# The low halves of the attention's weights, made on GpSimd in place of VectorE

## The chip, the core and the metric

The kernel runs on one core of a Trainium2 chip. The time is device time in microseconds (us), of whole executions. The engines are called by the profile's names: PE is TensorE's matmul (PEld its weight load), DVE is VectorE, ACT is ScalarE, POOL is GpSimd, SP is SyncE, which issues most loads. TensorE's granted clock stands as PEclk, 1.00 being 2.4 GHz.

## What is computed

Two transformer blocks, one behind the other, on 512 tokens of width 1024. The first has a convolution branch, a spatial gating branch and a mixture of 32 experts; the second has a feed-forward layer, a mixer of two attentions and a second feed-forward layer. The change touches the mixer of the second block alone:

```python
h = rmsnorm(x, g_mix[l])
p = h @ w_in[l]
qa, ka, va, qi, ki, wi, cq, ckv, kr = jnp.split(p, split_points, axis=-1)
...
out_a = dsa_sparse_attention(qa, ka, va, qi, ki, wi)
out_b = mla_attention(cq, ckv, kr, g_q_lat[l], g_kv_lat[l], w_uq[l], w_ukv[l], cos_b, sin_b)
x = x + jnp.concatenate([out_a, out_b], axis=-1) @ w_out[l]
```

The sparse attention (DSA) scores every earlier token with 16 small index heads, keeps the best 128 of them for each query, and attends to these alone. The latent attention (MLA) makes its queries, keys and values from two narrow projections (`cq`, `ckv`) and attends to all earlier tokens. Both outputs go through one projection.

## The kernel before

It is written in a tile framework: the program calls operations on named tiles, the framework finds the dependences, sets the waits and puts each engine's instructions into one order at build time, mostly that of the program, with later work moved ahead where a planner expects an engine to be free. On the chip each engine runs its queue strictly in that order.

**Split products.** A matmul in single pass rounds its operands. To keep accuracy, an operand is split into a high half (rounded) and a low half (the rest), and a product is three matmuls (`mm3`, lines 254 to 259): low by high, high by low, high by high, in this order. `hilo` (L201) makes the halves: ACT copies the source into the rounded type (L203, CAST in the profile), then DVE subtracts that from the source (L204). The same two lines serve weights and activations; in the profile the weights' halves are the tiles `wh` and `wl`, the activations' are called `t`.

**Weight stream.** `Stream` (L87) walks over a list of weight tiles: it lets SP load raw tiles four ahead of their use, and calls `wtile` (L219) two ahead, which takes a `wh` and a `wl` buffer (three of each, L128) and calls `hilo`. So the cast of a tile waits until PE is done with the tile three places before.

**The attention** (`attention`, L1209) runs these stages. The first stream (`st`, L1222) has 20 tiles: one of the key projection, eight for the index queries (1040 columns each, two to a group of heads), seven for keys and latents, four for the sparse attention's queries (1024 columns). The row scales come from `rms` (L326, with `rsqrt`, L261). For each group of index heads, `project`, `rotate` (rotary, L1274 to 1286) and `score_qi` (L1317) follow; `score_qi` adds the heads' scores up with one DVE instruction for each head and block (L1329). Then come the latent projections (L1353), the value projection with a tile of its own (L1398), and the stream `st2` (L1412) with 12 narrow tiles (four of 256, eight of 384 columns) for the MLA heads. `heads` (L1563) runs eight heads of one kind: scores with mask and maximum on DVE (L1520), exponentials on ACT (L1524), transposes and copies (L1537 to 1542), products with the values (L1550).

`choose` (L1453) finds the best 128 scores in 16 rounds of two DVE instructions (L1458, L1459). The order puts many of them early, as filling between other DVE work. `project_out` (L1477) takes the eight tiles of the output projection from the stream `st3` (L1475): four of them, for the MLA half, in between the last rounds, the others two by two at the end (L1498, L1499). The second feed-forward layer begins right behind, with a stream of its own.

Of the kernel before, what the change touches and what calls it, by code (L numbers as in the profile page):

```python
# [7 lines left out]
F32 = mybir.dt.float32  # L8
# [3 lines left out]
ALU = mybir.AluOpType  # L12
# [63 lines left out]
class Blocks:  # L76


    def __init__(self, tiles, n, w=512):
        self.tiles, self.n, self.w, self.per = tiles, n, w, 2048 // w  # L80
# [37 lines left out]
class Net:  # L118
    def __init__(self, tc, ctx, A, out):
        self.tc, self.nc, self.A, self.out, self.ctx = tc, tc.nc, A, out, ctx  # L120
        nc = self.nc
        ec = ctx.enter_context
        self.own = None
        self.const = ec(tc.tile_pool(name="const", bufs=1))
        self.p8 = ec(tc.tile_pool(name="p8", bufs=16))
        self.p4 = ec(tc.tile_pool(name="p4", bufs=4))
        self.p2 = ec(tc.tile_pool(name="p2", bufs=5))
        self.wp = ec(tc.tile_pool(name="wp", bufs=3))  # L128
        self.sm = ec(tc.tile_pool(name="sm", bufs=2))
        self.pp = ec(tc.tile_pool(name="pp", bufs=8, space=PSUM))  # L130
        self.dr = ec(tc.tile_pool(name="dr", bufs=1, space=DRAM))
        c = self.const
        self.x = c.tile([128, ND, T], F32, name="x")
        self.vec = c.tile([128, NV], F32, name="vec")
        nc.scalar.dma_start(self.vec, A["vec"])
        self.cc = c.tile([128, NC_], F32, name="cc")
        nc.scalar.dma_start(self.cc, A["cc"])
        self.ident = self.cc[:, C_ID:C_ID + 128]
        self.ones = c.tile([128, 128], F32, name="ones")
        nc.vector.memset(self.ones, 1.0)  # L140
        self.table = self.dr.tile([ROUNDS * 128 * NE, 4], I32, name="table")
        self.ordd = self.dr.tile([1, NE], I32, name="ordd")
        self.hrow = self.dr.tile([T, D], F32, name="hrow")
        self.pay = c.tile([128, NT, 2, 4], I32, name="pay")
        self.br = c.tile([128, NG + NE], F32, name="br")
        self.order = c.tile([128, NE], I32, name="order")
        self.payf = c.tile([128, NT, NFIXED, 4], F32, name="payf")
        self.payi = c.tile([128, NT, 2], F32R, name="payi")
        self.g12 = c.tile([128, ND], F32, name="g12")
        o1, o2 = VOFF["norm_final_g"], VOFF["g_ffn1_2"]  # L150
        nc.vector.tensor_tensor(self.g12, self.vec[:, o1:o1 + ND], self.vec[:, o2:o2 + ND], op=ALU.mult)
# [46 lines left out]
    def blocks(self, n, dt=F32, w=512):  # L198
        return Blocks([self.t8([128, 2048], dt) for _ in range(-(-n * w // 2048))], n, w)

    def hilo(self, hi, lo, src):  # L201
        nc = self.nc
        nc.scalar.copy(hi, src)  # L203
        nc.vector.tensor_tensor(lo, src, hi.bitcast(F32), op=ALU.subtract)  # L204

    def half(self, hi, lo, src, g):

# [11 lines left out]
    def wtile(self, view):  # L219

        shape = list(view.shape)
        if self.own is not None:
            wh, wl = (w.rearrange("p a b -> p (a b)").rearrange("p (a b) -> p a b", b=shape[2])
                      for w in self.own["w"].pop(0))
            self.hilo(wh, wl, view)
            return wh, wl
        wh = self.wp.tile(shape, F32R, name="wh", tag="wh")
        wl = self.wp.tile(shape, F32R, name="wl", tag="wl")
        self.hilo(wh, wl, view)
        return wh, wl  # L230

    def stream(self, items, loads=4, ahead=2):
# [976 lines left out]
    def attention(self):  # L1209
        nc, A = self.nc, self.A  # L1210
        mul, add, sub = ALU.mult, ALU.add, ALU.subtract
        def tok_items(nm, w, c):
            return [((nm, c), self.load8(w[c]), (lambda r, h=h: r[:, 4 * h:4 * h + 4, :])) for h in range(2)]
# [5 lines left out]
        items += self.stat_items("wf", wf, range(1, 8))  # L1219
        for c in range(2):  # L1220
            items += tok_items("qa", wqa, c)
        st = self.stream(items)  # L1222
        st.split(2)
        xh, xl = self.halves(lambda k: self.v("g_mix_2", k))
# [252 lines left out]
        def project_out(j, cs):  # L1477

            ws = [next(st3) for c in cs]
            accs = [self.ps() for m in range(2 * len(cs))]  # L1480
            for n, k in enumerate(ks[j]):
                for m, acc in enumerate(accs):
                    (wh, wl), o = ws[m // 2], slice(m % 2 * 128, m % 2 * 128 + 128)
                    self.mm3(acc, (wh[:, n, o], wl[:, n, o]), (mh[k], ml[k]), n == 0, n == 3)
            for m, acc in enumerate(accs):
                xm = self.x[:, 2 * cs[0] + m, :]
                nc.vector.tensor_tensor(xm, acc, xm, op=add)
# [9 lines left out]
        self.heads(dsa)  # L1497
        project_out(1, (0, 1))  # L1498
        project_out(1, (2, 3))  # L1499

    PO = [0, 128, 384, 768]
    SO = [0, 512, 896, 1152]
# [206 lines left out]
```

## Time and profile before

| | |
|---|---|
| median of three runs | 2027.65 us (2027.0 to 2028.92) |
| profiled execution, its own time | 2028.41 us |
| its span, first to last instruction | 2026.5 us |
| PE busy in the span | 1918.1 us, 95% |
| DVE busy | 1293.8 us, 64% |
| ACT busy | 715.6 us, 35% |
| POOL busy | 48.4 us, 2%, 69 instructions |
| mean granted clock | 0.978 |

The busy shares are means over stages that have little in common, so the attention has to be read by itself: how long each engine is busy in each of its stages, what PE waits for there, and where the subtractions stand in DVE's queue. A busy PE is one with at least one matmul under way; matmuls overlap, so that the step from one start to the next is shorter than one matmul's duration.

### The profile page before, as it was taken

The page shows a single profiled execution, that of the slowest core. Times are in us where ns is not written, and L with a number is a line of the kernel's source. Part 1 is how long each engine was busy: PE and PEld are TensorE (multiplying, and loading weights), DVE is VectorE, ACT ScalarE, POOL GpSimd, SP SyncE. Part 2 cuts the span into 40 slices and gives each one's busy share as a digit, 9 for nine tenths or more (in the row PEclk, how much of TensorE's full clock was granted, in tenths as well). Part 3 has the DMA queues.
Part 4 walks back from the last instruction along what each step waited for, and adds up shares of the span by engine and source line. Part 5 has one row for each costly group of instructions (what it writes and reads, how often), then busy time and mean ns, then how long its engine had stood idle before and what let it go on. Part 6 is the DMA issues. An engine that isn't in the chain of part 4 may idle for free.

```text
span 2026.5 us, 24440 instructions
## 1 busy us (share of the span) xinstructions
PE 1918.1 (95%) x9375; PEld 1428.8 (71%) x9375; DVE 1293.8 (64%) x2234; ACT 715.6 (35%) x1116; POOL 48.4 (2%) x69
## 2 busy tenths in 40 slices
PE   7999999979998899887999999999989999999997
PEld 5898888867554353332788888887867788888886
DVE  7999997457777575555754442459999755444323
ACT  5334325345343221111532322336366633223221
POOL 0000001003000000000000000000000000000000
PEclk9999999988999999999999999999999999999998
DMA  6121232527999999998232224130111122222311
GB/s 258 53 87 60 104 124 104 236 108 271 385 409 409 408 416 408 410 420 334 85 104 94 94 79 170 66 151 1 53 50 47 48 83 92 96 94 83 151 57 42
DMA packets 60087, 341.59 MB, mean 169 GB/s; under 512 B 8208, under 2 KB 9168, under 8 KB 27456
## 3 DMA queue, kind: packets, MB, share of 16 engines
q1 hardware_dynamic: 55152, 329.87, 42.2%
q0 software_dynamic: 3520, 6.35, 1.0%
q10 hardware_dynamic: 1296, 3.79, 0.5%
q8 instruction: 74, 1.21, 0.2%
q14 instruction: 45, 0.37, 0.1%
HBM read 339.37 MB, written 4.54 MB: 170 GB/s over the span
## 4 chain that ended last, share of the span: by engine, by line
PE 47%; DVE 3%; ACT 2%; issue 0%; DMA 0%; DVEq 0%; ACTq 0%; SPq 0%
PE ps L257 15%; PE ps L259 14%; PE ps L258 14%; PE ps L1550 1%; ACT t L1524 1%; PE ps L1537 1%; DVE wl L204 0%; DVE t L204 0%; PE ps L1292 0%; ACT wh L203 0%; PE ps L1555 0%; DVE t L1520 0%; ACT t L203 0%; PE ps L295 0%; PE ps L1293 0%
## 5 line engine op out<-in xcount | busy, mean ns | idle before, releaser
L257 PE MATMUL ps<-t,wl 128*128 128x512 f32 x1728 | 684.2, 397 | 18.7 <-ACT t L208 18.3
L258 PE MATMUL ps<-t,wh 128*128 128x512 f32 x1728 | 681.2, 394 | 0.9 <-DVE t L209 0.9
L259 PE MATMUL ps<-t,wh 128*128 128x512 f32 x1728 | 681.4, 394 | 0.0
L203 ACT CAST wh<-t 128x1024 fp32r<-128x1024 f32 (+3 forms) x321 | 324.9, 1017 | 716.9 <-PE ps L259 532.7
L204 DVE TENSOR_TENSOR wl<-t,wh 128x1024 fp32r<-128x1024 f32 (+3 forms) x321 | 378.3, 1183 | 212.0 <-ACT wh L203 208.8
L257 PEld LDWEIGHTS ps<-t,wl 128*128 128x128 f32 x1728 | 325.3, 188 | 96.9 <-ACT t L208 19.1
L258 PEld LDWEIGHTS ps<-t,wh 128*128 128x128 f32 x1728 | 326.0, 189 | 76.8 <-DVE t L209 2.3
L259 PEld LDWEIGHTS ps<-t,wh 128*128 128x128 f32 x1728 | 325.3, 188 | 75.4
L257 PE MATMUL ps<-wh,t 128*128 128x256 f32 (+2 forms) x440 | 147.4, 337 | 23.2 <-DVE t L204 23.2
L972 PE MATMUL ps<-t,t 128*32 128x512 f32 (+1 forms) x832 | 162.6, 606 | 5.5 <-DMA t<-in_w_up 3.6
L403 DVE SCALAR_TENSOR_TENSOR t<-t,vec,t 128x512 f32<-128x512 f32 x240 | 165.7, 745 | 0.4
L1025 DVE TENSOR_TENSOR x<-x,ps 128x512 f32<-128x512 f32 x200 | 126.4, 683 | 44.9 <-PE ps L1024 44.1
L258 PE MATMUL ps<-wl,t 128*128 128x256 f32 (+2 forms) x440 | 145.7, 331 | 0.0
L259 PE MATMUL ps<-wh,t 128*128 128x256 f32 (+2 forms) x440 | 144.4, 328 | 0.0
L257 PEld LDWEIGHTS ps<-wh,t 128*128 128x128 f32 x440 | 85.8, 195 | 33.0 <-DVE t L204 25.1
L972 PEld LDWEIGHTS ps<-t,t 128*32 128x32 f32 (+1 forms) x832 | 41.4, 123 | 91.7 <-issue 78.8
L1181 DVE TENSOR_TENSOR t<-ps,rbc 128x512 f32<-128x512 f32 x44 | 30.4, 690 | 115.6 <-PE ps L259 115.6
L259 PEld LDWEIGHTS ps<-wh,t 128*128 128x128 f32 x440 | 85.9, 195 | 7.4
L258 PEld LDWEIGHTS ps<-wl,t 128*128 128x128 f32 x440 | 86.0, 195 | 6.8
L1024 PEld LDWEIGHTS ps<-t,t 128*128 128x128 f32 x248 | 42.8, 190 | 67.1 <-issue 31.6
L1024 PE MATMUL ps<-t,t 128*128 128x512 f32 x248 | 78.7, 424 | 11.5 <-DVE t L1012 7.4
L203 ACT CAST t<-t 128x512 fp32r<-128x512 f32 (+2 forms) x102 | 62.7, 619 | 57.5 <-DVE t L1182 26.2
(317 smaller groups left out, 1597.1 us busy)
## 6 DMA issues: line engine op xcount, KB each, us to landing
t<-in_w_down SPq DMA_DIRECT2D x80, 1024.0 KB, 19.8
t<-in_w_gate SPq DMA_DIRECT2D x64, 1024.0 KB
t<-in_w_up SPq DMA_DIRECT2D x64, 1024.0 KB, 19.2
t<-in_w_in SPq DMA_DIRECT2D x24, 1024.0 KB, 4.7
t<-in_w_gate SPq DMA_DIRECT2D x44, 512.0 KB
t<-in_w_up SPq DMA_DIRECT2D x44, 512.0 KB, 3.4
t<-in_w_down SPq DMA_DIRECT2D x8, 768.0 KB, 11.4
t<-in_w_qi SPq DMA_DIRECT2D x4, 1040.0 KB, 4.7
```

The source lines that it names most:

```text
L203: nc.scalar.copy(hi, src)
L204: nc.vector.tensor_tensor(lo, src, hi.bitcast(F32), op=ALU.subtract)
L257: mm(acc, a[1], b[0], start=first, stop=False)
L258: mm(acc, a[0], b[1], start=False, stop=False)
L259: mm(acc, a[0], b[0], start=False, stop=last)
L403: nc.vector.scalar_tensor_tensor(y[c], src, w, y[c], op0=mul, op1=add)
L972: nc.tensor.matmul(p[o:o + c, :], xT[:, k * CAP + i:k * CAP + i + c], w[:, q, :], start=k == 0, stop=k == ND - 1)
L1024: self.nc.tensor.matmul(p, yT[:, k * 128:k * 128 + 128], sel, start=j == 0, stop=j == n - 1)
L1025: self.nc.vector.tensor_tensor(self.x[:, k, :], self.x[:, k, :], p, op=ALU.add)
L1181: nc.vector.tensor_tensor(a, accs[1], rbc, op=mul)
L1524: nc.scalar.activation(part(i), part(i), AF.Exp, bias=nm[:, i:i + 1], scale=scale, accum_out=su[:, i:i + 1])
L1537: nc.tensor.transpose(tb[b][:, o + (i - s) * 128:o + (i - s) * 128 + 128], P[:, self.PO[i] + s * 128:self.PO[i] + s * 128 + 128], self.ident)
```

## The change

`hilo` gets an argument for the engine that makes the low half; only `wtile` passes one, from a field of the net. `attention` sets the field to GpSimd ahead of its first stream and clears it at its end, so that the 41 weight tiles of the attention (20 of the first stream, the value projection's one, 12 narrow ones and eight of the output projection) have their low halves made there. The casts stay on ACT, and the activations' low halves on DVE. All other streams of the kernel are as before.

```diff
@@ -118,6 +118,7 @@
 class Net:
     def __init__(self, tc, ctx, A, out):
         self.tc, self.nc, self.A, self.out, self.ctx = tc, tc.nc, A, out, ctx
+        self.low = None
         nc = self.nc
@@ -198,10 +199,10 @@
-    def hilo(self, hi, lo, src):
+    def hilo(self, hi, lo, src, low=None):
         nc = self.nc
         nc.scalar.copy(hi, src)
-        nc.vector.tensor_tensor(lo, src, hi.bitcast(F32), op=ALU.subtract)
+        (low or nc.vector).tensor_tensor(lo, src, hi.bitcast(F32), op=ALU.subtract)
@@ -226,7 +227,7 @@
         wl = self.wp.tile(shape, F32R, name="wl", tag="wl")
-        self.hilo(wh, wl, view)
+        self.hilo(wh, wl, view, self.low)
         return wh, wl
@@ -1219,6 +1220,7 @@
         for c in range(2):
             items += tok_items("qa", wqa, c)
+        self.low = nc.gpsimd
         st = self.stream(items)
         st.split(2)
@@ -1497,6 +1499,7 @@
         project_out(1, (0, 1))
         project_out(1, (2, 3))
+        self.low = None
```

## Rows read from the trace of the kernel before

**Rows 1.** Busy time by stage (stretch, length, then each engine, clock, DMA).

```profile
core 0: us, PE busy (x) PEld busy (x) DVE busy (x) ACT busy (x) POOL busy (x), PEclk, DMA share, GB/s
1300.00:1350.00 50.00, 50.00 (x252) 42.23 (x252) 22.37 (x26) 18.64 (x24) 0.00 (x0) 1.00 0.33 126
1350.00:1430.00 80.00, 73.72 (x444) 63.31 (x443) 71.46 (x146) 43.87 (x95) 0.00 (x0) 0.98 0.13 51
1430.00:1480.00 50.00, 49.85 (x333) 44.91 (x333) 48.13 (x137) 15.81 (x25) 0.00 (x0) 1.00 0.04 12
1480.00:1550.00 70.00, 60.80 (x333) 47.38 (x333) 66.08 (x171) 55.77 (x133) 0.00 (x0) 0.95 0.15 49
1550.00:1585.00 35.00, 34.94 (x193) 27.13 (x191) 31.82 (x82) 13.22 (x30) 0.00 (x0) 1.00 0.19 69
```

**Rows 2.** Waits, 1350 to 1585 us: us in total, times, the longest.

```profile
PE ps L257 <- DVE t L204: 7.1, 3, 4.7
...
DVE wl L204 <- ACT wh L203: 4.6, 6, 1.6
```

**Rows 3.** Groups by line and shape, DVE, 1325 to 1645: busy, mean ns.

```profile
L204 DVE TENSOR_TENSOR wl<-t,wh 128x1024 fp32r<-128x1024 f32 x23 | 28.0, 1219 | 7.7 <-ACT wh L203 7.5
...
L204 DVE TENSOR_TENSOR wl<-t,wh 128x384 fp32r<-128x384 f32 x8 | 4.4, 552 | 0.6 <-ACT wh L203 0.6
```

**Rows 4.** DVE's busy time on the weights' low halves alone, by stage.

```profile
1350.00:1430.00 80.00, 11.08 (x9) 0.98 0.13 51
1430.00:1480.00 50.00, 9.46 (x9) 1.00 0.04 12
1480.00:1550.00 70.00, 7.80 (x13) 0.95 0.15 49
1550.00:1585.00 35.00, 4.66 (x4) 1.00 0.19 69
```

**Rows 5.** Groups by line and shape, POOL, whole span.

```profile
L565 POOL TENSOR_SCALAR t<-t,vec 128x36 f32<-128x36 f32 x8 | 2.8, 365 | 2.2 <-DMA t<-in_w_router 2.2
...
L559 POOL MEMSET t<- 128x2048 f32 x1 | 1.8, 1810 | 22.3 <-DVE wl L204 22.3
...
L391 POOL MEMSET t<- 128x96 f32 x3 | 0.6, 186 | 38.6 <-DVE t L376 28.3 <-DVE wl L204 10.3
...
L669 POOL CAST ur<-ones 128x128 fp32r<-128x128 f32 x1 | 0.3, 292 | 0.0
```

**Rows 6.** Timeline of ACT in the score stage: start, us.

```profile
1360.64 1.06 ACT L203 CAST wh<-t 128x1040 fp32r<-128x1040 f32 x1 [0.62 <-PE ps L259]
...
1364.97 1.07 ACT L203 CAST wh<-t 128x1040 fp32r<-128x1040 f32 x1 [1.21 <-PE ps L259]
```

**Rows 7.** Timelines of DVE and PE at the last weight tile.

```profile
1632.48 1.22 DVE L204 TENSOR_TENSOR wl<-t,wh 128x1024 fp32r<-128x1024 f32 x1
...
1633.84 0.47 PE L257 MATMUL ps<-t,wl 128*128 128x512 f32 x1
```

**Rows 8.** Timeline of DVE in the chain of the row scales.

```profile
1351.32 1.24 DVE L204 TENSOR_TENSOR wl<-t,wh 128x1040 fp32r<-128x1040 f32 x1
1352.48 0.17 DVE L269 RECIPROCAL r<-rs 128x4 f32<-128x4 f32 x1
1352.68 0.16 DVE L270 TENSOR_TENSOR rt<-r 128x4 f32<-128x4 f32 x1
```

**Rows 9.** Timeline of all engines, 339 us, in the first block.

```profile
339.05 0.75 DVE L482 SCALAR_TENSOR_TENSOR t<-ps,vec,t 128x512 f32<-128x512 f32 x1
339.27 0.29 POOL L668 CAST ur<-cc 128x128 fp32r<-128x128 f32 x1 [13.90 <-ACT t L203]
```

**Rows 10.** Groups by line, DVE, 1350 to 1585 us: those with two SBUF inputs.

```profile
L1329 DVE SCALAR_TENSOR_TENSOR t<-t,wb,t 128x256 f32<-128x256 f32 (+2 forms) x45 | 24.6, 614 | 0.3 <-ACT t L1326 0.2
...
L204 DVE TENSOR_TENSOR t<-t,t 64x512 fp32r<-64x512 f32 (+2 forms) x22 | 15.0, 681 | 0.2
L1280 DVE TENSOR_TENSOR t<-t 128x256 f32<-128x256 f32 x20 | 8.4, 418 | 0.1
```

## The prediction

> **What bounds the kernel now.** I read the views in this order: the busy time by stage, the waits of the attention, the weights' rows on VectorE (DVE), and then single stretches of the timeline. The attention runs from about 1350 to 1645 us, and its first two weight tiles are made a little earlier. Up to 1350 TensorE (PE) never stops: 50.00 busy of 50.00 us, with DVE at 22.37. Nothing that DVE gives up there can be worth anything. Behind that the picture changes [rows 1]. PE stands for 80 - 73.72 = 6.28 us in the score stage (1350 to 1430), for 0.15 us in the stage of the latent projections (1430 to 1480), for 9.20 us in that of the MLA heads (1480 to 1550) and for 0.06 us while the top-k choice and the first part of the output projection run (1550 to 1585). DVE is full in all four: 71.46 of 80, 48.13 of 50, 66.08 of 70, 31.82 of 35. GpSimd (POOL) does nothing in any of them.
>
> So PE is the bound of the attention as a whole, and DVE is what makes it stand in two stages. The largest wait of PE is on a DVE subtraction: 7.1 us in three pieces, 4.7 the longest [rows 2]. The 16 us of PE's idle time are all that a faster DVE can ever give back, 0.8% of the run.
>
> **What the change removes.** Every weight tile of the attention is split by a cast on ScalarE (ACT) and a subtraction, the low half, on DVE. A tile of 1024 columns costs DVE 1219 ns, one of 384 costs 552 ns [rows 3]. By stage that is 11.08, 9.46, 7.80 and 4.66 us [rows 4], together 33.0 of DVE's 217.5 us in the four. With it goes a second cost: the subtraction stands in DVE's queue before its cast is ready, and all behind it waits too, 4.6 us in six pieces [rows 2]. I put these into the score stage whole, which then gives back 11.08 + 4.6 = 15.7 us of DVE. The other subtractions of the same line (those of the activations) stay on DVE.
>
> **What it adds.** The same 41 subtractions on POOL. No row shows a POOL instruction with two tensor inputs, so its price is bounded by four others [rows 5]. The two memsets (186 ns for 96 columns, 1810 for 2048) give 0.83 ns a column and 0.106 us fixed: at least 0.96 us for 1024 columns, which only writes. The cast of 128 columns takes 292 ns, so (292 - 106) / 128 = 1.45 ns a column; it reads once and writes in the same type as the low half, and is the nearest row. If the second input costs nothing more, a tile takes 0.106 + 1.49 = 1.6 us; if it costs as much again, 3.1. I take the middle, 2.3 us, and keep 1.6 to 3.1. The far end is the 36-column product at 365 ns: (365 - 106) / 36 = 7.2 ns a column, 7.5 us a tile; most of it must be fixed cost, so I keep it only for a rival. In the Trainium skill, "GPSIMD Engine Reference", section 3.1, a two-input operation on 2048 columns is put at 4497 ns; an estimate from that is 2.25 us for 1024, and with it the sum below would not move. No run here shows it.
>
> **Where it lies.** POOL has no other work and no DMA to issue in the attention, so no queue is passed there. What waits is PE, whose first product of a tile reads the low half. ACT starts a new cast when PE lets a tile go, here at 1360.64 and 1364.97 [rows 6]; tiles have three buffers, so PE is two tiles, some 8.7 us, away from the new one. Cast (1.07) and subtraction (2.3) leave 5.3 us of cover, and the step costs nothing as long as that holds. The raw tile is let go about 1.1 us later, and SyncE's next load of it with it; loads run four tiles ahead, at a DMA share of 0.04 to 0.19 [rows 1], and hide that. If they didn't, a tile would come 1.1 us late.
>
> One place has no cover. The last weight tile of the output projection is cast only when the tile three before it is free; its subtraction starts on DVE at 1632.48 and ends at 1633.70, and PE's next product starts at 1633.84 with a longer step than its neighbours' [rows 7]. With 2.3 us that becomes **+1.1 us** on PE.
>
> **What the time gained is worth if POOL runs freely beside DVE.** At 1351.32 a subtraction stands in the chain that makes the row scales, for which PE waits: the reciprocal comes right behind it, at 1352.48 [rows 8]. Without it the chain is some 1.0 us shorter. The rest of the score stage gives DVE back more than PE stands idle (15.7 against 6.28 less that 1.0), but part of that idle time is made by ACT; I take 3 us of the 5.3. In the MLA stage DVE gets back 7.80 us, about one part in nine of its time, and PE stands 9.20; the waits also run through casts and exponentials on ACT, so I take 5. In the two other stages PE is full: 0. Sum: -1.0 - 3 - 5 + 1.1 = **-7.9 us**.
>
> **And if they get in each other's way.** Both engines read the same tile memory. What the trace has of this is one-sided: a POOL cast beside a DVE instruction with one input in that memory and one from PSUM kept 0.29 us, and DVE 0.75 [rows 9]. A DVE instruction with two inputs in the tile memory beside a reading POOL one is not in the trace long enough to show anything. Three kinds of those, the score sums (L1329), the subtractions of activations and the rotary sum (L1280), make 24.6 + 15.0 + 8.4 = 48 us in 87 instructions [rows 10]. Without the removed ones DVE has 217.5 - 33.0 = 184.5 us of work, so it meets one every 2.1 us, and on the average 1.06 us after a POOL subtraction has started. If it then waits for that to end, a wide tile costs DVE 2.3 - 1.06 = 1.24 us: just what was saved. Narrow tiles (0.93 us by the same price) are done before. The score stage has nine wide tiles: 11.2 of 15.7 us are lost again, 29% stay, worth 0.9 of the 3 us. The MLA stage has three wide and ten narrow ones: 3.7 of 7.8 are lost, 53% stay, worth 2.6 of the 5. The chain of row scales now loses: its first two-input step, at 1352.68 [rows 8], would wait for 1351.32 + 2.3 = 1353.62, +0.9. Sum: -0.9 - 2.6 + 0.9 + 1.1 = **-1.5 us**.
>
> The Trainium skill, "SBUF — State Buffer", section "Who interferes with whom", says that a VectorE instruction with two SBUF inputs contends with a GpSimd instruction that reads SBUF, that the pair of ports is an exclusive lock for a whole instruction, and that the later one blocks fully. By that rule this case holds and the free one falls; no run here shows it yet, and the one overlap above, with a single SBUF input, agrees with it.
>
> **The forecast** is the second case. Rows do not refuse the first, but it needs both unknowns to fall well, a price below 2.3 us or no meeting at all; the second stands in the middle of the bounds. The profiled execution took 2028.41 us, 1.9 more than its span of 2026.5, and lies 0.76 above the median of the runs, 2027.65. The sum against it is 2026.9, and against the median 2027.65 - 1.5 = 2026.1.
>
> **Rivals.**
> - *POOL runs freely beside DVE:* 2027.65 - 7.9 = 2019.7. For it: POOL is empty, PE has two tiles of lead, and no overlap in the trace slows anyone. Against it: no row has two-input work on both engines.
> - *POOL holds DVE up for longer than it relieves it* (the other side). The place is the score stage, where two-input instructions stand in long runs. It decides from a block of 15.7 / 9 = 1.74 us a wide tile, thus a price of 2.8 us. At 3.1 us the block is 2.04: nine tiles lose 18.4 against 15.7, +2.7; the MLA stage is even; the chain of row scales loses 1351.32 + 3.1 - 1352.68 = 1.7, the last tile 1.9. Sum +6.3: 2034.
> - *POOL becomes the bound:* at 7.5 us a tile against the 4.3 us in which PE uses one up, the eight wide tiles of the index queries alone cost 8 x 3.2 = 25 us: 2053. Only the 36-column row speaks for it, the cast against it.
> - *The change does not do what it says* (subtractions stay on DVE): 2027.65. Only the field that the tile maker reads is set, and it is cleared behind the last tile, so I see little room.
>
> The program's order is made when it is built, and a moved filler (a replace step of the choice, some 0.7 us) ahead of a chain may cost or give a few of its own lengths; I allow 2 us either way.
>
> **How the numbers follow.** Forecast 0.40, free running 0.32, held up 0.20, POOL the bound 0.05, nothing done 0.03. A difference below 0.2%, 4.1 us, can hardly be told from no change. Faster: nearly all of free running (0.30) and the lower edge of the forecast (0.07), 0.37. Slower: most of held up (0.17), POOL the bound (0.05) and an edge of the forecast (0.02), 0.24. The rest, 0.39, is within. The range goes from 2017 (free running with 2 us and a little more of PE's idle time) to 2036 (held up, plus 2); left out are POOL as the bound and some of each end, together under 0.2. The forecast's own range is 2023 to 2030.
>
> **What would show it.** In the new profile POOL should have 41 subtractions, near 2.3 us for 1024 columns; DVE's busy time in the four stages, taken with its blocked time, shows the relief, by -33 if it is free. Two-input rows of DVE (L1329, 0.61 us in the mean) that have grown, or gaps ahead of them while POOL is busy, show the blocking. PE's idle time should fall by 2 to 4 us in the MLA stage and little in the score stage, and the product at 1633.84 should come about 1 us late. The forecast is wrong if L1329 keeps its length beside busy POOL (free running), if a wide tile takes over 2.8 us, or if PE waits on the low half anywhere but at the last tile.

## The result, and the profile after

The changed kernel takes 2047.3 us (median, 2044.61 to 2051.15) against 2029.66 us (2027.0 to 2031.68) of the kernel before beside it: a ratio of 1.0089, 95% interval 1.0079 to 1.0100. It is 18 us slower. The prediction was 2026.1 us, with a range from 2017 to 2036. The profiled execution took 2046.8 us, with a span of 2044.7.

Behind line 204 the lines of the changed kernel are numbered one higher than before, in the attention two or three. Where the time went is read from five marks in the timeline of PE: the first product of the index queries (260 columns wide), the first product of the row scales, the first MLA score, the first DSA value product, and the end.

| stretch | before, us | after, us | PE idle in it, before and after |
|---|---|---|---|
| start to first index-query product | 1341.39 | 1342.06 | |
| to the row scales | 12.11 | 13.06 | 2.52, 3.47 |
| to the first MLA score ("score stretch") | 139.78 | 150.27 | 8.66, 15.84 |
| to the first DSA value product ("MLA stretch") | 98.10 | 103.22 | 4.70, 7.63 |
| to the end | 435.16 | 436.07 | 11.05, 12.01 |

The attention and what follows took 685.15 us before and take 702.61 now, 17.5 more. 10.5 of these lie in the score stretch. About two thirds are added idle time of PE; the rest is PE working longer, at a lower granted clock.

Busy time by stage after [rows 1] (columns as there; the last stretch here is 50 us long, and the borders no longer meet the same work):

```profile
1300.00:1350.00 50.00, 50.00 (x250) 42.11 (x249) 19.65 (x22) 18.73 (x24) 11.96 (x5) 1.00 0.33 122
1350.00:1430.00 80.00, 67.94 (x417) 60.15 (x416) 72.00 (x131) 41.23 (x92) 22.49 (x10) 0.94 0.09 32
1430.00:1480.00 50.00, 50.00 (x316) 44.76 (x315) 47.81 (x132) 14.72 (x22) 17.71 (x8) 0.99 0.11 45
1480.00:1550.00 70.00, 58.72 (x319) 46.01 (x319) 67.11 (x168) 50.16 (x115) 16.61 (x13) 0.95 0.14 47
1550.00:1600.00 50.00, 47.19 (x254) 36.57 (x250) 24.91 (x65) 22.02 (x54) 9.88 (x4) 0.93 0.15 52
```

From 1350 to 1430 us DVE is busy for 72.00 us, where it was 71.46, although its nine subtractions of weights are gone: fewer instructions, some of them far longer. PE fell from 73.72 to 67.94. The groups by line and shape of POOL, 1300 to 1665 us, show that the change did what it says [rows 3 and 5]:

```profile
L205 POOL TENSOR_TENSOR wl<-t,wh 128x1024 fp32r<-128x1024 f32 x21 | 51.9, 2472 | 615.5 <-ACT wh L204 615.5
L205 POOL TENSOR_TENSOR wl<-t,wh 128x1040 fp32r<-128x1040 f32 x8 | 19.5, 2444 | 24.4 <-ACT wh L204 24.4
L205 POOL TENSOR_TENSOR wl<-t,wh 128x384 fp32r<-128x384 f32 x8 | 9.2, 1153 | 36.5 <-ACT wh L204 36.5
L205 POOL TENSOR_TENSOR wl<-t,wh 128x256 fp32r<-128x256 f32 x4 | 2.9, 736 | 16.2 <-ACT wh L204 16.2
```

There are 41 subtractions, 2.47 us for 1024 columns where 2.3 were taken. The groups of DVE by line, 1350 to 1600 us, answer [rows 10]:

```profile
L1331 DVE SCALAR_TENSOR_TENSOR t<-t,wb,t 128x256 f32<-128x256 f32 (+2 forms) x45 | 27.4, 675 | 0.6 <-ACT t L1328 0.4
...
L1282 DVE TENSOR_TENSOR t<-t 128x256 f32<-128x256 f32 x20 | 17.5, 873 | 0.1
L205 DVE TENSOR_TENSOR t<-t,t 64x512 fp32r<-64x512 f32 (+2 forms) x22 | 17.2, 785 | 2.4 <-ACT t L204 2.0
...
L1354 DVE TENSOR_TENSOR t<-t 32x512 f32<-32x512 f32 x1 | 2.5, 2489 | 0.3 <-ACT t L1353 0.3
```

The same instructions on the same tiles take longer: the score sum 675 ns (614 before), the activations' low half 785 (681), the rotary sum 873 (418). One rotary sum that had no reason to last over 0.7 us lasts 2.49. The timeline shows why. DVE (start, duration):

```profile
1352.13 0.18 DVE L270 RECIPROCAL r<-rs 128x4 f32<-128x4 f32 x1 [0.29 <-ACT rs L269]
1352.34 2.12 DVE L271 TENSOR_TENSOR rt<-r 128x4 f32<-128x4 f32 x1
...
1436.32 2.49 DVE L1354 TENSOR_TENSOR t<-t 32x512 f32<-32x512 f32 x1 [0.30 <-ACT t L1353]
...
1470.87 0.41 DVE L1276 TENSOR_TENSOR t<-ps,t 128x256 f32<-128x256 f32 x1
1471.20 1.88 DVE L1282 TENSOR_TENSOR t<-t 128x256 f32<-128x256 f32 x1
1473.00 0.28 DVE L1280 TENSOR_TENSOR t<-ps,t 128x128 f32<-128x128 f32 x1
```

POOL at the same places, and at the last weight tile:

```profile
1352.07 2.37 POOL L205 TENSOR_TENSOR wl<-t,wh 128x1040 fp32r<-128x1040 f32 x1 [1.87 <-ACT wh L204]
...
1435.85 2.41 POOL L205 TENSOR_TENSOR wl<-t,wh 128x1024 fp32r<-128x1024 f32 x1 [13.16 <-ACT wh L204]
...
1470.38 2.41 POOL L205 TENSOR_TENSOR wl<-t,wh 128x1024 fp32r<-128x1024 f32 x1 [3.29 <-ACT wh L204]
...
1649.59 2.45 POOL L205 TENSOR_TENSOR wl<-t,wh 128x1024 fp32r<-128x1024 f32 x1 [46.62 <-ACT wh L204]
```

A product of 128 x 4 numbers (L271) that starts at 1352.34 ends at 1354.46, with POOL's subtraction (1352.07 + 2.37 = 1354.44). The rotary sum that starts at 1471.20, while POOL is at work until 1472.79, ends 0.29 us behind it. The product right before it (L1276, one input from PSUM) keeps its 0.41 us beside the same subtraction. From 1300 to 1680 us 25 instructions of DVE are lengthened in this way, by 31.8 us in all (each against the median of its kind in the trace of before).

### The profile page after: what moved, and what is told of

Same layout as the page of the kernel before. It is cut to its first block, busy times and chain, and to the rows that moved or that the text cites. A ratio compares the mean times of both kernels' runs of the same rounds, so it can differ in the third digit from the quotient of the medians.

```text
span 2044.7 us, 24471 instructions
## 1 busy us (share of the span) xinstructions
PE 1924.1 (94%) x9375; PEld 1433.6 (70%) x9375; DVE 1287.0 (63%) x2193; ACT 715.6 (35%) x1116; POOL 134.1 (7%) x110
## 5 line engine op out<-in xcount | busy, mean ns | idle before, releaser
L205 DVE TENSOR_TENSOR wl<-t,wh 128x1024 fp32r<-128x1024 f32 (+1 forms) x280 | 336.7, 1207 | 193.5 <-ACT wh L204 191.7
L258 PEld LDWEIGHTS ps<-t,wl 128*128 128x128 f32 x1728 | 326.0, 189 | 98.1 <-ACT t L209 19.7
L259 PE MATMUL ps<-wl,t 128*128 128x256 f32 (+2 forms) x440 | 145.9, 332 | 0.0
L205 POOL TENSOR_TENSOR wl<-t,wh 128x1024 fp32r<-128x1024 f32 (+3 forms) x41 | 83.5, 2040 | 692.6 <-ACT wh L204 692.6
```

What stands on the lines that cost most here:

```text
L205: (low or nc.vector).tensor_tensor(lo, src, hi.bitcast(F32), op=ALU.subtract)
L258: mm(acc, a[1], b[0], start=first, stop=False)
L259: mm(acc, a[0], b[1], start=False, stop=False)
```

## The experiments

Each kernel was timed beside the kernel before on one chip. "Attention" is the time from the first index-query product to the end in the profiled execution, 685.15 us before and 702.61 after; the two stretches are those of the table above. "Lengthened" is the sum over DVE's instructions, 1300 to 1680 us.

| kernel | median us | ratio, 95% interval | attention | score stretch | MLA stretch | lengthened |
|---|---|---|---|---|---|---|
| changed kernel | 2047.30 | 1.0089 (1.0079 to 1.0100) | 702.6 | 150.3 | 103.2 | 31.8 |
| write_only | 2025.92 | 0.9963 (0.9949 to 0.9977) | 681.3 | 136.5 | 98.5 | 0.4 |
| choice_as_before | 2042.11 | 1.0051 (1.0034 to 1.0068) | 695.9 | 143.6 | 103.2 | 34.4 |
| choice_early | 2046.79 | 1.0069 (1.0052 to 1.0086) | 702.3 | 156.1 | 98.6 | 0.0 |
| extra_reader | 2050.25 | 1.0089 (1.0072 to 1.0105) | 705.6 | 155.2 | 100.8 | 30.1 |
| extra_write | 2030.82 | 1.0003 (0.9994 to 1.0012) | 684.7 | 139.8 | 98.1 | 1.2 |
| mla_part_only | 2037.01 | 1.0036 (1.0023 to 1.0049) | 692.6 | 142.0 | 102.5 | 4.9 |
| score_stage_only | 2046.15 | 1.0069 (1.0056 to 1.0081) | 702.9 | 153.4 | 101.2 | 17.9 |
| out_projection_only | 2038.10 | 1.0038 (1.0026 to 1.0050) | 693.8 | 141.3 | 104.2 | 6.1 |
| one_read | 2025.67 | 0.9979 (0.9970 to 0.9988) | 680.7 | 135.0 | 98.9 | 3.1 |
| score_psum | 2038.63 | 1.0040 (1.0026 to 1.0054) | 694.4 | 148.4 | 96.9 | 11.5 |
| psum_alone | 2039.33 | 1.0041 (1.0028 to 1.0054) | 693.7 | 145.9 | 100.3 | 0.0 |
| in_pieces | 2038.52 | 1.0040 (1.0027 to 1.0052) | 693.4 | 145.2 | 100.0 | 15.1 |

write_only, choice_as_before, choice_early and extra_reader stood beside runs of the kernel before with a median of 2032.32 us, the changed kernel beside 2029.66, the others beside medians of 2029.76 to 2030.73; the ratios take that out.

**write_only.** The order of PE and DVE is that of the changed kernel.

```diff
-            low.tensor_tensor(lo, src, hi.bitcast(F32), op=ALU.subtract)
+            low.memset(lo.bitcast(F32), 0.0)
```

> The changed kernel, but GpSimd fills the low half with zeros in place of subtracting: it writes the tile and reads nothing (the low halves of the attention's weights are left out of the result). The order of the instructions on DVE, PE and ACT is that of the changed kernel, and so 72 of the choice's 96 instructions still stand ahead of the first MLA score. Theory 1 (the chip holds DVE's two-input instructions up while GpSimd reads): L1331 falls back to 614 ns from 675, the rotary sum to 418 from 873, and the time to 2018 to 2030. Theory 2 (the new order, with 11 us more of the choice ahead of the MLA heads, makes the loss): the time stays at 2038 to 2047.

0.9963, 7.5 us faster than before. With POOL as busy in the same places, but reading nothing, the loss is gone and turns into a gain. The interval of the ratio puts it between 4.6 and 10.4 us; in the profiled execution the attention is 3.9 us shorter. Two groups of DVE, 1350 to 1600 us, and timelines of DVE and POOL:

```profile
L1334 DVE SCALAR_TENSOR_TENSOR t<-t,wb,t 128x256 f32<-128x256 f32 (+2 forms) x45 | 24.6, 613 | 0.6 <-ACT t L1331 0.4
...
L1285 DVE TENSOR_TENSOR t<-t 128x256 f32<-128x256 f32 x20 | 8.3, 418 | 0.1
...
1386.87 0.41 DVE L1285 TENSOR_TENSOR t<-t 128x256 f32<-128x256 f32 x1
...
1386.51 0.96 POOL L206 MEMSET wl<- 128x1024 f32 x1 [10.01 <-PE ps L263]
```

The score sum and the rotary sum are back at their lengths of before, and one rotary sum keeps 0.41 us inside a POOL instruction of 0.96 us. A fill is shorter than a subtraction, though, so this run alone does not tell reading from length.

**choice_as_before and choice_early.** When the program was built, the order of DVE changed with the relief. Of the 96 instructions of the top-k choice (MAX8 and MATCH_REPLACE8), 50 start in the score stretch before and 71 after. The first run puts them back in the changed kernel, the second brings them forward in the kernel before.

```diff
-            choose(r)
+            if r < 8:
+                choose(r)
+            else:
+                with self.tc.issue_after(self.marks[0].ins):   # first head's nm
+                    choose(r)
```

> The changed kernel, with rounds 8 to 15 of the choice queued behind the first MLA head on DVE: 48 of its instructions stand ahead of the first MLA score, as against 50 in the kernel before and 72 in the changed one. Theory 1 (blocking): the blocked time stays, 2042 to 2048. Theory 2 (order): the first MLA score comes some 11 us earlier than in the changed kernel, 2032 to 2038. Both at work: in between.

```diff
+        for r in range(12):
+            choose(r)
         self.heads(mla)
         for r in range(TOPK // 8):
-            choose(r)
+            if r >= 12:
+                choose(r)
```

> The kernel before, all subtractions on DVE, with rounds 0 to 11 of the choice put ahead of the MLA heads in the program: 78 of its instructions stand ahead of the first MLA score. Theory 1 (blocking): nothing blocks here, 2026 to 2033. Theory 2 (order): the MLA heads start some 14 us late and the time does not come back, 2036 to 2044.

1.0051 and 1.0069. In the changed kernel the order makes 0.38%, about 8 of the 18 us, all in the score stretch (150.3 to 143.6 us). The other 10 us stay without it. On a DVE that is not relieved the early choice alone (78 instructions) costs 14 us; in write_only, with 71 instructions early, it costs nothing that shows. I read this as follows: the order is a loss because the room that was planned for it did not come.

**extra_reader.** The kernel before, in its own order; POOL repeats the subtraction, and no result depends on it.

```diff
         self.hilo(wh, wl, view)
+        if self.low is not None:
+            self.low.tensor_tensor(view, view, wh.bitcast(F32), op=ALU.subtract)
```

> The kernel before in its own order on DVE, PE and ACT, all subtractions on DVE, and as an addition GpSimd subtracts the same operands again into the raw tile, which nobody reads: the blocking without the relief, and PE waits for none of it. Theory 1 (blocking): DVE loses some 24 us more in its full stages, 2040 to 2055. Theory 2 (order): order and relief are those of before, 2027 to 2034.

1.0089: the whole loss of the changed kernel, with nothing taken from DVE and nothing moved. Groups by line of DVE (1350 to 1600 us) and of POOL:

```profile
L1284 DVE TENSOR_TENSOR t<-t 128x256 f32<-128x256 f32 x20 | 14.1, 705 | 0.1
...
L232 POOL TENSOR_TENSOR t<-t,wh 128x1024 f32<-128x1024 f32 (+3 forms) x41 | 83.5, 2037 | 698.7 <-DVE wl L205 620.5 <-ACT t L1330 24.0 <-issue 17.3
```

**extra_write.** The same place, but a fill in place of the subtraction.

```diff
-            self.low.tensor_tensor(view, view, wh.bitcast(F32), op=ALU.subtract)
+            self.low.memset(view, 0.0)
```

> The kernel before in its own order, VectorE still makes every low half; GpSimd then fills the raw view, once its readers are done, with a constant (41 fills in the places of the 41 added subtractions of the kernel extra_reader, same tiles, same engine, no SBUF operand read). Theory 1 (what costs time is GpSimd reading two SBUF operands while VectorE wants to read two as well): within 3 us of the kernel before, ratio 0.9985 to 1.0015, no VectorE instruction of two SBUF operands over 1.2 times its length in the kernel before. Rival (any work of GpSimd on the raw tiles costs the time, because the tile's buffer comes free later and the next load with it, or because GpSimd touches SBUF at all): as extra_reader, ratio 1.007 to 1.011.

1.0003 (0.9994 to 1.0012). Neither POOL's presence nor the raw tile's later release costs anything that can be measured, as far as a fill of 0.96 us shows it; the subtraction keeps the tile 1.5 us longer. In extra_reader, where it does so, no instruction waits for a DMA from 1300 to 1660 us, so the later release does not show there either.

**mla_part_only, score_stage_only, out_projection_only.** POOL takes only the tiles from the MLA heads' stream on, only those ahead of it, or only the eight of the output projection.

```diff
-        self.low = nc.gpsimd
         st = self.stream(items)
...
+        self.low = nc.gpsimd
         st2 = self.stream(items)
```

> The changed kernel with the GpSimd subtraction only for the weight tiles from the MLA heads' stream on (uk, uq and the output projection), VectorE for all of the score stage. Theory 1 (blocking at the places where a two-operand VectorE instruction lies on the chain that TensorE waits for): the score stage is as before, 139.8 us from the row-scale rows to the first MLA score; the MLA part gets 2 to 5 us longer, as the part from the first MLA score to the first DSA value product did in the changed kernel (98.1 to 103.2 us); ratio 1.000 to 1.003. Rival (in the MLA part VectorE has much work and the relief, 12.5 us by two rows of the kernel before, is larger than the blocking, 3 to 4 us): ratio 0.997 to 0.999, and this is then the version that beats both.

> The changed kernel with the GpSimd subtraction only for the weight tiles ahead of the MLA heads' stream (wf, qi, qa, uv), VectorE for uk, uq and the output projection. Theory 1: the score stage keeps its added 10 us (139.8 to about 150), the last weight tile's 0.9 us and the MLA part's 5 us are gone; ratio 1.005 to 1.008. Rival (the loss is spread over both parts alike, or the score stage's loss is given back in the MLA part because more of the choice is done early): ratio 1.000 to 1.004.

> The changed kernel with the GpSimd subtraction only for the 8 tiles of the output projection (4 of them beside the rounds of the choice, which are MAX8 and MATCH_REPLACE8 and are not lengthened in the changed kernel). VectorE makes all others; the order of the choice is that of the kernel before (50 of 96 ahead of the first MLA score). Theory 1: relief of 8 x 1.2 us = 10 us of VectorE in a part where it meets few two-operand instructions: ratio 0.998 to 1.0005, with about +1 us at the last tile on GpSimd. Rival (blocking in the DSA heads, whose score and product instructions read SBUF): ratio 1.001 to 1.003.

1.0036, 1.0069 and 1.0038. Both parts lose, the score stage twice as much. The ratio of the score part agrees with theory 1, but its MLA stretch is still 3.1 us longer than before (101.2 us) with no subtraction of POOL in it: 2.4 of these are PE working longer, 95.7 us in place of 93.4 at a granted clock of 0.94 in place of 0.97. The other two are worse than theory 1 said, and the output projection was a miss of both theories: eight moved tiles cost 7.7 us. Its timelines (DVE, POOL, PE) and the busy time of one stretch show how:

```profile
1548.38 2.79 DVE L1448 TENSOR_TENSOR t<-t,t 32x512 f32<-32x512 f32 x1
...
1552.38 1.58 DVE L208 TENSOR_TENSOR t<-t,t 96x512 fp32r<-96x512 f32 x1
...
1548.18 5.23 POOL L208 TENSOR_TENSOR wl<-t,wh 128x1024 fp32r<-128x1024 f32 x2 [9.45 <-ACT wh L207]
...
1551.56 0.44 PE L261 MATMUL ps<-t 96*128 96x384 f32 x1 [2.97 <-DVE mx L1526]
...
1554.02 0.47 PE L261 MATMUL ps<-t 96*128 96x128 f32 x1 [1.49 <-DVE t L208]
...
1550.00:1560.00 10.00, 6.95 (x28) 5.79 (x30) 8.81 (x31) 5.14 (x16) 3.41 (x2) 0.66 0.32 107
```

The first three tiles are made ahead, beside the last MLA head. Two subtractions back to back (5.23 us) hold two instructions of the head's query chain for 2.1 and 0.9 us. PE stands 2.97 and 1.49 us for that chain. Its granted clock, 1.00 in the ten us before, is 0.66 in these, a mean of the two levels 2.4 and 1.2 GHz; before it was 1.00 in both stretches. The tiles beside the choice, where I expected the relief, cannot pay: PE is busy for 10.00 of 10 us there.

**one_read.** The changed kernel; POOL copies the raw tile and does not read the high half.

```diff
-            low.tensor_tensor(lo, src, hi.bitcast(F32), op=ALU.subtract)
+            low.tensor_copy(lo, src)
```

> The changed kernel in its own order on TensorE and VectorE; GpSimd makes the 41 low halves as a plain copy of the raw tile in place of the subtraction, so it reads one SBUF operand and not two (the high half isn't subtracted: that part of the computation is left out). Theory 1 as it stands (two operands on one side against two on the other): as write_only, ratio 0.995 to 0.998, VectorE's instructions at their lengths of the kernel before. Rival (any read of GpSimd holds VectorE's two-operand instructions back, for as long as the copy lasts): VectorE lengthened as in the changed kernel, ratio 1.003 to 1.009.

0.9979 (0.9970 to 0.9988), 4.3 us faster than before. The time agrees with theory 1; its mechanism does not. POOL and DVE in the timeline:

```profile
1384.22 1.04 POOL L206 CAST wl<-t 128x1024 fp32r<-128x1024 f32 x1 [9.91 <-PE ps L263]
...
1384.57 0.96 DVE L1285 TENSOR_TENSOR t<-t 128x256 f32<-128x256 f32 x1
...
1521.37 0.68 DVE L1449 TENSOR_TENSOR t<-t,t 32x512 f32<-32x512 f32 x1
...
1521.47 1.49 POOL L206 CAST wl<-t 128x1024 fp32r<-128x1024 f32 x1 [3.35 <-PE ps L261]
```

The rotary sum ends at 1385.53, 0.27 us behind the copy (1385.26), as it would behind a subtraction: one operand read by POOL is enough. And it goes both ways: a copy that starts 0.10 us after a DVE instruction lasts 1.49 in place of 1.05 us and ends 0.91 us after it. The copy costs little because it lasts 1.05 us, not 2.47, so it is met less often and left sooner (3.1 us lengthened).

**score_psum and psum_alone.** The score sum and the rotary sum get one input from PSUM; once in score_stage_only, once in the kernel before.

```diff
-                    t = self.t2()
-                    nc.scalar.activation(t[:, 0:e], p[:, 0:e], AF.Relu)
+                    t = p
+                    nc.scalar.activation(t[:, 0:e], p[:, 0:e], AF.Relu)
...
-                nc.vector.tensor_tensor(a.rearrange(c8, d=32), acc[:, 0:256].rearrange(c8, d=32), ...
-                nc.vector.tensor_tensor(a, a, b, op=add)
+                nc.vector.tensor_tensor(a0.rearrange(c8, d=32), a0.rearrange(c8, d=32), ...   # a0 = acc[:, 0:256]
+                nc.vector.tensor_tensor(a, a0, b, op=add)
```

> The kernel score_stage_only with the two groups of VectorE instructions that were lengthened most beside PE's waits changed to one SBUF operand: the relu of the index scores is left in PSUM, where the accumulation reads it, and the rotary sum reads its first term from PSUM. Theory 1 (the blocking of these instructions is what the score stage loses): VectorE's accumulations and rotary sums keep their lengths (about 0.6 and 0.4 to 0.5 us), the score stage goes from 153 to 140-146 us, ratio 0.998 to 1.003. Rival (the score stage is long because of the order of the choice and the clock behind the idle time, whatever is blocked): still 1.005 to 1.008.

> The kernel before, VectorE makes every low half, with the same two edits (relu left in PSUM, rotary sum with one term from PSUM). It is the base for score_psum: both theories expect 0.997 to 1.003 of it; the score stage is 138 to 142 us. If it is much faster or slower than the kernel before, score_psum is to be read against it and not against the kernel before.

1.0040 and 1.0041. The two edits cost 0.4% of their own, outside what both theories gave them, so score_psum is read against psum_alone: the same move of subtractions that cost 0.69% on the kernel before costs nothing here in sum. The score stretch, expected at 140 to 146 us, is 148.4, which is 2.5 more than psum_alone's 145.9 (the move cost 13.6 there without the edits); the MLA stretch is 3.4 shorter. In score_psum the rotary sum is back at its length beside 21 subtractions of POOL (groups by line and shape, DVE, 1350 to 1600 us):

```profile
L1283 DVE TENSOR_TENSOR t<-ps,t 128x256 f32<-128x256 f32 x20 | 8.4, 418 | 0.3
```

Why the edits cost 0.4% alone was not followed up.

**in_pieces.** The changed kernel with each low half in pieces; the order of PE and DVE is unchanged.

```diff
+        m = 4 if n % 4 == 0 else n
+        for j in range(m):
+            c = slice(j * n // m, (j + 1) * n // m)
+            low.tensor_tensor(lo[:, c], src[:, c], hi[:, c].bitcast(F32), op=ALU.subtract)
```

> The changed kernel, its order on TensorE and VectorE unchanged; GpSimd makes each low half in pieces (a tile of 1024 in four of 256, at about 736 ns each by the changed kernel's trace, so 2.9 us a tile in place of 2.47). If a VectorE instruction of two SBUF operands waits only for the GpSimd instruction that is at work, it now waits at most 0.74 us where it waited up to 2.4: the 31.8 us by which VectorE's instructions were lengthened fall to 8 to 15 us, the score stage goes from 150 to 142-146 us, ratio 1.000 to 1.005; the last tile and the row-scale chain pay 0.4 us more each. Rival (GpSimd's pieces follow each other without letting VectorE in, so a VectorE instruction waits for all the pieces of a tile): lengthening as before or more (30 us and up), ratio 1.009 to 1.013.

1.0040, and 15.1 us lengthened in place of 31.8: less than half, though POOL reads for longer. POOL and DVE in the row-scale chain:

```profile
1356.38 2.80 POOL L212 TENSOR_TENSOR wl<-t,wh 128x260 fp32r<-128x260 f32 x4 [1.51 <-ACT wh L204]
...
1356.65 0.47 DVE L278 TENSOR_TENSOR rt<-r 128x4 f32<-128x4 f32 x1
1357.16 0.65 DVE L279 TENSOR_TENSOR rt<-rt,var 128x4 f32<-128x4 f32 x1
1357.85 0.66 DVE L280 TENSOR_SCALAR rt<-rt 128x4 f32<-128x4 f32 x1
1358.55 0.65 DVE L281 TENSOR_TENSOR rtok<-r,rt 128x4 f32<-128x4 f32 x1
```

Four instructions of 0.16 us each wait for one piece each and get in between two pieces. So DVE waits for one POOL instruction, not for the whole tile. What is left at 1.0040 (8 us) was not split between the remaining waits and the early choice.

No version beat both kernels. The two that were faster than the kernel before leave the subtraction out.

## Why the prediction was wrong, point by point

**What holds.** The change does what it says, POOL is not the bound, and its price was near (2.47 for 2.3 us). The mechanism of the forecast, DVE blocked by POOL, is shown: with reads 18 us slower, with the same order and no reads 7.5 faster, with reads and nothing else 18 slower. The chain of the row scales was put at +0.9 and took +0.95 (12.11 to 13.06). The last tile was put at +1.1: PE's idle time ahead of it is 0.95 us, and the rest of the kernel 0.9 us longer.

```profile
1652.09 0.50 PE L258 MATMUL ps<-t,wl 128*128 128x512 f32 x1 [0.95 <-POOL wl L205]
```

**The step that failed: 1.24 us for a wide tile, from one two-input instruction every 2.1 us.** The 2.1 us are a mean over four stages, and nine of the wide tiles lie in the stage where these instructions are densest. Groups by line of DVE before, 1350 to 1430 us alone [rows 10]:

```profile
L1329 DVE SCALAR_TENSOR_TENSOR t<-t,wb,t 128x256 f32<-128x256 f32 (+2 forms) x45 | 24.6, 614 | 0.3 <-ACT t L1326 0.2
...
L1280 DVE TENSOR_TENSOR t<-t 128x256 f32<-128x256 f32 x12 | 5.0, 419 | 0.1
...
L204 DVE TENSOR_TENSOR t<-t,t 128x512 fp32r<-128x512 f32 x2 | 1.4, 683 | 0.0
```

59 of the 87 instructions stand here, in 71.46 - 11.08 = 60.4 us of DVE's work: one every 1.02 us. By the forecast's own rule a wide tile then costs 2.3 - 0.51 = 1.79 us, and nine cost 16.1, more than the 15.7 that the stage gives back. The runs show this: all nine wide tiles of the stage from 1350 to 1430 us blocked something, 1.96, 2.03, 2.25, 1.31, 0.81, 2.10, 0.83, 2.01 and 2.10 us, 15.4 in all, 1.71 a tile. The rival "held up" was to begin at 1.74; it spoke of long runs of these instructions in this stage but did not count them. The narrow tiles, put at nothing, blocked five times as well, 0.5 to 0.7 us each.

Five of the nine are a rotary sum or the first product of the row scales, and four of these start within 0.5 us of POOL. The two may not be independent: PE's last product with a tile lets go of its buffer, so that ACT casts and POOL subtracts, and it also finishes the accumulator that DVE then rotates. No run moved the one event against the other, and the spacing in the stage gives the size without it, so this part is not shown; the sizes of the blocks are measured.

**The second failed step: lost time counted like regained time.** Blocks as large as the relief would leave the score stage even; it lost. The forecast took a fraction of DVE's net relief (29% in the score stage, 53% in the MLA stage) as PE's gain. The relief was spent on the choice, which no one waits for yet (71 instructions in the score stretch, 38.1 us of DVE, in place of 50 and 27.0). The blocks fell on the rotation, the key and the latent chain, for which PE waits next. Waits of the changed kernel, 1350 to 1600 us (us, times, longest) [rows 2]:

```profile
PE ps L258 <- DVE t L205: 6.7, 3, 4.3
...
PE ps L258 <- DVE mx L1523: 4.5, 6, 1.2
PEld ps L1284 <- DVE t L1282: 4.4, 5, 2.2
...
PE ps L296 <- DVE rtok L274: 3.5, 1, 3.5
```

The old wait is still there (7.1 before), and the rotary sum now stands beside it. So where the terms -0.9 and -2.6 stood, the score stretch took +10.5 and the MLA stretch +5.1. The borders differ: the forecast's MLA stage begins at 1480 us, 13 us before the first MLA score, and 4.0 of the 10.5 lie behind the first product of the last row scales (1474.05 before, 1482.10 after). 2.2 of the 5.1 are PE working longer. Five blocks of 0.5 to 1.8 us also fell into the stage of the latent projections, which had been put at 0 because PE never stood there.

**The MLA term was too large in the free case as well.** It took 5 us of gain out of 9.20 us of idle time. Half of these are one wait, right before the first MLA score, for a low half of activations (tile `t`), which the change leaves on DVE. PE in the kernel before, in write_only and in one_read:

```profile
1493.28 0.33 PE L257 MATMUL ps<-t 96*128 96x128 f32 x1 [4.74 <-DVE t L204]
...
1491.42 0.47 PE L261 MATMUL ps<-t 96*128 96x128 f32 x1 [4.29 <-DVE t L208]
...
1489.16 0.33 PE L261 MATMUL ps<-t 96*128 96x128 f32 x1 [4.27 <-DVE t L208]
```

The wait hardly reacts. Behind it, the MLA stretch is 98.5 us in write_only and 98.9 in one_read against 98.1: PE's idle time there falls from 4.70 to 3.96 and 4.50, its work grows by 1.1 and 1.0 at a lower granted clock, and nothing is gained, though DVE had 11.5 us of subtractions and 21 instructions of the choice less to do. The score stretch, which includes that wait, gave 3.3 and 4.7 us (the score stage was put at 3), the row-scale chain 1.0 in both, as forecast. By the traces of these two kernels the attention is 3.9 and 4.5 us shorter, so the free case's -7.9 was nearly twice too large, and the 7.5 us in write_only's ratio do not confirm its working.

**The allowance of 2 us for the order.** It was worth 8, because the change moves the balance by which the order is planned: 21 of the 96 choice instructions went to another stage, not one filler.

**The rivals.** "Held up" had the right sign and place. Its price was too small, +6.3, for the same reason as the forecast's: it counted only the surplus of blocks over relief. That the clock would fall in PE's new idle stretches stood in no case: PE worked 3.3 us longer in the score stretch and 2.2 in the MLA stretch on the same products; of the latter, 1.0 to 1.1 are there in write_only and one_read too. Granted clock by stretch, after (columns as in [rows 1]):

```profile
1410.00:1420.00 10.00, 9.69 (x48) 7.84 (x47) 9.56 (x18) 6.29 (x14) 0.13 (x1) 1.00 0.01 2
1420.00:1430.00 10.00, 7.38 (x25) 5.88 (x24) 9.95 (x15) 5.13 (x13) 2.69 (x1) 0.69 0.23 80
```

PE stands for 2.62 us here. The block passes through three engines: POOL's subtraction holds the second rotary sum of the key (L1244, 2.79 in place of 0.68 us), ACT's cast of the key waits 2.81 us for it, and the relus that PE waits for stand behind that cast in ACT's queue. The clock falls from 1.00 to 0.69. In write_only the score stretch has 129.1 us of PE's work, in the changed kernel 134.4.

## What to carry to other kernels

Before work moves from VectorE to GpSimd, list what VectorE runs beside each moved instruction, and count the two-input ones in that stage alone; a mean over stages hides the dense one. Relief counts where it falls, on fillers as a rule; a block counts where it falls, and if that is a chain that TensorE waits for, it costs its full length, and the slower clock behind the gap on top. Two kernels settle such a case cheaply: the new order without the suspected conflict, and the conflict alone in the old order.

## What the runs showed of the hardware

- A GpSimd instruction that reads tile memory and a VectorE instruction with two inputs in tile memory do not run at the same time. Whichever starts second ends behind the first by its own length less 0.13 to 0.21 us in the blocks that the tables count (a block of several pieces in a row aside), as if it had only begun to work near the first one's end: 0.28 us behind for a rotary sum of 0.42, 0.54 for a sum of 0.68, 1.08 for VectorE's own subtraction of 1.22 in extra_reader, 0.91 for GpSimd's copy of 1.05. One rotary sum took 1.88 us in this way, the copy 1.49. One operand read by GpSimd is enough. A fill of 0.96 us, which reads nothing, delayed no VectorE instruction with two such inputs.
- The Trainium skill, "SBUF — State Buffer", section "Who interferes with whom", says just this: a contest with a GpSimd instruction that reads, not with one that only writes, an exclusive lock for a whole instruction, decided by who issues first. For instructions with two inputs the runs agree with it in each point; the prediction cited it and went wrong on how often the two meet and on what that delays, not on the rule.
- Size does not matter to the loser: a product of 128 x 4 numbers (0.16 us) took 2.12 us. VectorE's products of one tensor in tile memory with a constant (TENSOR_SCALAR) wait too, and even for a fill: 0.66 in place of 0.17 us beside the pieces, 1.19 in place of 0.35 beside a fill in extra_write. MAX8, MATCH_REPLACE8 and the instructions with an input from PSUM kept their lengths.
- A GpSimd subtraction takes 2.47 us for 1024 columns, 1.15 for 384 and 0.74 for 256 (VectorE: 1.22 and 0.55 for the first two); a copy of 1024 takes 1.07, a fill 0.95.
